# A one-core hybrid attention layer: all fetches that ScalarE issued are issued by GpSimd, and the gate's weights come in two transfers

## The chip, the cores and the metric

The kernel runs on one core of a Trainium2 chip. The metric is the device time of one execution in microseconds (us). Each version was run several times; the median counts. One execution was also taken by the hardware profiler, and the views quoted below come from it. Engines are named as in the profile: PE is TensorE's matmul, PEld its weight load, DVE is VectorE, ACT is ScalarE, POOL is GpSimd and SP is SyncE. ACTq, SPq and POOLq are the queues in which an engine issues DMAs. L145 means line 145 of the kernel.

## The reference

One layer of a model with 256 tokens of width 2048, all in fp32. The input is projected by one wide matrix; from its columns come three groups of dilated local attention (8 heads of width 128 each, with a learned bias by distance) and a gated linear attention (4 heads, decay gates from a low-rank product). Both are projected, gated, added and projected again; then a layer norm, a feed-forward part with a short convolution (width 5632), and another layer norm.

```python
parts = jnp.split(x @ w_in, cuts, axis=-1)
gq, gk, gv, gr, g_low, m_a, m_b = parts[3 * N_GROUPS:]
...
    o, lse = _dilated_group(qg, kg, vg, rel_bias[:, g * A_HEADS:(g + 1) * A_HEADS], dil)
...
ya = ya.reshape(b, s, A_WIDTH).astype(x.dtype) @ w_proj_a
log_a = jax.nn.log_sigmoid((g_low @ gla_gate_w + gla_gate_b).astype(jnp.float32)) / G_TAU
o = _gla(gq.reshape(b, s, G_HEADS, G_HK) * (G_HK ** -0.5), ..., log_a.reshape(b, s, G_HEADS, G_HK))
yb = (o.reshape(b, s, G_DV).astype(x.dtype) * jax.nn.silu(gr)) @ w_proj_b
y = jax.nn.sigmoid(m_a) * ya + jax.nn.sigmoid(m_b) * yb
return y @ w_out
```

`gla_gate_w` has 16 rows and 1024 columns: it takes the 16 low-rank columns `g_low` to the 1024 decay gates.

## The kernel before

**Weights.** The weights stream in tiles of 128 x 1024 fp32 (512 KB), issued by SP in `load` (L154). Each tile is split into two parts that TensorE takes at its faster fp32 format: ACT copies it to `whi` (L145), and DVE subtracts that copy from it to give `wlo` (L146). Every product is then three matmuls. In most places the tile is called `raw`; in the units below it is called `quarter`.

**Units.** A part of the big projection is computed with Strassen's scheme (the function around L331): seven products, named by letters after the unit's name (vA is the product A of unit v), over sums and differences of quarters of the weight matrix. The quarters are added in two ways: on DVE (L356, "quarter<-quarter,quarter"), and by a DMA that adds into its destination, issued by POOL (`add_by_dma`, L358-359, "quarter<-quarter", 120 of them). A product takes four weight tiles, four "chunks" of six matmuls. Between units stand ordinary projections, such as `gqk` or `qk` (L236 for `whi`, L238 for `wlo`).

**Side work.** Beside the stream run two lists of small stages, `side` (an attention head's steps) and `slow` (the gated linear attention), which `pump` (L194) takes up between the weight tiles. A head's `bias` (L459) fetches its bias table from DRAM in four transfers of 32 rows; `values` (L523) fetches `v`, three transfers from the buffers `vs` to which units spilled their output; `low_loads` (L584) fetches the low-rank weights: `glr`, and the gate's weights `gws`. Those lie in two tiles of 80 rows, in which rows 0-15, 32-47 and 64-79 each hold the same 16 rows of weights and the rows between are zero; so POOL clears each tile (L594) and three transfers of 16 rows fill it. `low_rank` (L615) copies its result `gl` to two more places by DMA; `get` (L666) fetches `gc` and `gq`, `att` (L711) fetches `gv`, and before the last down projection the four tiles of `acc` are fetched (L1213).

**Who issues.** In the kernel before, all these fetches are issued by ACT, `fetch` (L115) with `by=nc.scalar`. For `fetch` and `v` the issue is tied behind the newest `whi` (L120, L527, `newest` set at L145). All other fetches and all spills (L112, L573) are issued by POOL; SP issues the weight stream and the loads at the start. A scheduler decides the order of each engine's instructions from the program, and each engine then runs its own list in order: an instruction behind a DMA issue on the same engine starts only when that issue has gone out. An issue waits for the data it reads, for its destination to be free, and for one of eight slots: SP and ACT share eight, POOL has eight of its own, and the ninth issue waits until the first has landed.

Of the kernel before, what the change touches and what calls it, by code (L numbers as in the profile page):

```python
# [25 lines left out]
RANK = 16  # L26
# [34 lines left out]
def hybrid_layer(ctx: ExitStack, tc: tile.TileContext, wp, xt, wgl, gw, par, relb, onehot, rows, xk, out):  # L61
    nc = tc.nc
# [49 lines left out]
        nc.gpsimd.dma_start(d, src)  # L112
        return d

    def fetch(name, d, make=None, by=None):  # L115
        b = (make or blk)(name)
        if by is None:
            nc.gpsimd.dma_start(b, d)
        else:
            with tc.issue_after(newest[0].ins):  # L120
                by.dma_start(b, d)
        return b

    def few(name, n, bufs=4):
# [17 lines left out]
    newest = []  # L142
# [312 lines left out]
    def attend(h, qk):  # L455

        st = {}

        def bias():  # L459
            T = big("bias", (3, S))  # L460
            r = bvd[h]
            for q in range(0, P, 32):
                src = bass.AP(r.tensor, r.offset + 127 - q, [[383, 32], [32 * 384, 3], [1, S]])
                nc.scalar.dma_start(T[q : q + 32], src)
            st["T"] = T

        def scores(g):
            def f():
                if not g:
                    st["s"] = blk("s0")[:, :384], big("s1", (768,))  # L470
                q, k = qk[g][:, :S], qk[g][:, S:]
                ps = bank("ps")
                pts = []
                for t in range(2):
                    n = (t + 1) * P
                    pts.append(ps[:, t * P : t * P + n])
                    nc.tensor.matmul(pts[t], q[:, t * P : (t + 1) * P], k[:, :n], start=True, stop=True)
                for t, pt in enumerate(pts):
                    n = (t + 1) * P
                    s = st["s"][t][:, g * n : (g + 1) * n]  # L480
                    nc.vector.scalar_tensor_tensor(s, pt, scale, st["T"][:, g, S - n :], op0=ALU.mult, op1=ALU.add)
            return f

        def soft(t):
            def f():
                s = st["s"][t]
                nm = few("nm", 1)
                nc.vector.tensor_reduce(nm, s, axis=AX.X, op=ALU.max, negate=True)
                l = few("l", 1)
                nc.scalar.activation(s, s, AF.Exp, bias=nm, accum_out=l)  # L490
                rl = few("rl", 1)
                nc.vector.reciprocal(rl, l)
                nc.vector.tensor_scalar_mul(s, s, rl)
            return f

        def turn(g):
            def f():
                pt = bank("ppt")
                s0, s1 = st["s"]
                nc.tensor.transpose(pt[:, 0:P], s0[:, g * P : (g + 1) * P], ident)  # L500
                for kt in range(2):
                    c = g * S + kt * P
                    nc.tensor.transpose(pt[:, (kt + 1) * P : (kt + 2) * P], s1[:, c : c + P], ident)
                p = blk("pT")[:, :384]
                nc.scalar.activation(p, pt[:, :384], AF.Copy)
                st["p", g] = p
            return f

        def mix(g):
            def f():  # L510
                if not g:
                    st["po"] = bank("po")[:, :S]
                po, p = st["po"], st["p", g]
                v0, v1 = (st["v"][:, g, t] for t in range(2))
                nc.tensor.matmul(po, v0, p[:, :S], start=(g == 0), stop=False)
                nc.tensor.matmul(po[:, P:], v1, p[:, S:], start=False, stop=(g == 2))
                if g == 2:
                    y = tmp("ya")
                    nc.scalar.activation(y, po, AF.Copy)
                    YA[h] = spill("yas", y)  # L520
            return f

        def values():  # L523
            st["v"] = big("v", (3, 2, HD))
            for g in range(3):
                src = VS[g][h // 4][:, :, (h % 4) * HD : (h % 4 + 1) * HD]
                with tc.issue_after(newest[0].ins):  # L527
                    nc.scalar.dma_start(st["v"][:, g], src)

        idle = lambda: None  # L530
        return bias, [scores(g) for g in range(3)], [soft(0), soft(1), idle, ("values", values), turn(0), turn(1), mix(0), turn(2), mix(1), idle, mix(2)]


    VS = [[dpool.tile([P, 2, 512], F32, name=f"vs_{g}_{half}") for half in range(2)] for g in range(3)]
    GKQ = [[None] * GH for _ in range(2)]
    GV, GR = ([[None] * 2 for _ in range(GH)] for _ in range(2))
# [46 lines left out]

    def low_loads():  # L584
        glr = tmp("glr")
        nc.scalar.dma_start(glr, wgl)


        places = [slice(r, r + RANK) for r in (0, 32, 64)]
        stack = slice(0, 64 + RANK)  # L590
        gws = []
        for j in range(2):
            w = blk("gws")
            nc.gpsimd.memset(w[stack], 0.0)  # L594
            for r in places:
                nc.scalar.dma_start(w[r], gw[:, j * 512 : (j + 1) * 512])
            gws.append(w)
        gl = tmp("gl")
        nc.gpsimd.memset(gl[stack], 0.0)
        low.update(gws=gws, gl=gl, glr=glr, stack=stack, places=places)  # L600
# [14 lines left out]
    def low_rank():  # L615
        gl, stack, places = low["gl"], low["stack"], low["places"]
        glh, gll = low["parts"]
        pg = bank("pgl")
        for kc in range(16):
            w = slice(kc * RANK, (kc + 1) * RANK)  # L620
            xo = xop(kc)
            nc.tensor.matmul(pg[:RANK], glh[:, w], xo, start=(kc == 0), stop=False)
            nc.tensor.matmul(pg[:RANK, S:], gll[:, w], xo[:, :S], start=False, stop=(kc == 15))
        nc.scalar.activation(gl[:RANK], pg[:RANK, :S], AF.Copy)
        nc.vector.tensor_tensor(gl[:RANK], pg[:RANK, S:], gl[:RANK], op=ALU.add)
        for r in places[1:]:
            nc.scalar.dma_start(gl[r], gl[:RANK])

    def low_parts():
        gl, stack, places = low["gl"], low["stack"], low["places"]  # L630
# [15 lines left out]
    def gla(h):  # L646
# [17 lines left out]
            DEC[h] = spill("gcs", c)  # L664

        def get():  # L666
            st["c"] = fetch("gc", DEC[h], by=nc.scalar)
            st["q"], st["k"] = (fetch("gq", GKQ[i][h], by=nc.scalar) for i in (1, 0))

        def decay():  # L670
            c = st["c"]
# [39 lines left out]
        def att():  # L711
# [14 lines left out]
                av, av, [[0, 2], [1, P]], ALU.is_ge, 0.0, base=0, channel_multiplier=-1  # L726
            )
            st["a"] = a
            st["gv"] = [fetch("gv", d, by=nc.scalar) for d in GV[h]]

        def outs():
            a, gv = st["a"], st["gv"]
# [453 lines left out]
    for part, nf in enumerate(FSPLIT):  # L1186
# [19 lines left out]
        if nf == 4:  # L1206
            rows2 = [res("ln2", F32) for _ in range(2)]
            G2, B2 = ([row(i, n, rows2[i][:, n]) for n in range(4)] for i in range(2))
            acc = res("acc", F32)
            for n in range(2):  # L1210
                for t in range(2):
                    F[t][n] = acc[:, 2 * t + n]
                    nc.scalar.dma_start(F[t][n], ACC[t][n])  # L1213
        older = down_group(part, nf, [h() for h in hs])
    act_set(ACT_LN_EXP, held_by[0])
    norm = [mean_and_scale(t) for t in range(2)]
# [115 lines left out]
def _layout(i):  # L1332
# [9 lines left out]
        "wp": np.stack([_by_rows(f(w)[0][r : r + n], c, m) for w, r, n, c, m in STREAM]),  # L1342
        "xt": f("x")[0].T.reshape(16, P, S).transpose(1, 0, 2).reshape(P, 16 * S),
        "wgl": _by_rows(w_in, C_GL, RANK),
        "gw": f("gla_gate_w")[0],
        "par": par,
        "relb": np.concatenate([f("rel_bias"), np.ones((1, 24), np.float32)]),
        "onehot": _bucket_rows(),
# [22 lines left out]
```

## Time and profile before

| what | value |
|---|---|
| timed runs, us | 1867.16, 1867.26, 1864.41; median 1867.16 |
| span of the profiled execution, us | 1866.8 |
| queue of SP (hardware), MB, share of 16 DMA engines | 345.09, 51.6% |
| queue of POOL (software), MB, share | 118.62, 25.6% |
| queue of ACT (hardware), MB, share | 13.21, 2.2% |
| DMA issues on ACT's queue | `bias` 32, `v` 24, `gq` 8, `gv` 8, `gws` 6, `gc` 4, `acc` 4, `gl` 2, `glr` 1, and the output |

The profiled execution carries no time of its own beside its span, so the span is set against the median of the timed runs: it lies 0.36 us below it. The profile gives, for each engine, what it did and what ended the idle time before an instruction (the "releaser"). A granted clock of 1.00 is TensorE's full rate; at 0.50 each matmul takes twice as long. Busy shares are means over the span; what a change is worth in one place is read from the timelines of that place.

### The profile page before, as it was taken

Reading aid. Unit: us, or ns where it says so; the run is one execution under the profiler, and the core shown is the slowest. Engines: PE = TensorE matmul, PEld = TensorE weight load, DVE = VectorE, ACT = ScalarE, POOL = GpSimd, SP = SyncE. Lnnn points to the kernel's source line nnn. Section 1 sums busy time; section 2 is a strip of 40 time slices with the busy share of each in tenths; the row PEclk is TensorE's granted clock in tenths of the full one; section 3 lists DMA queues with packets and bytes.
Section 4 is the critical chain, followed back from the end, with each engine's and each line's share of the span. In section 5 each row is a group of like instructions: output and inputs, shape, how many; then the busy total and the mean of one; then the engine's idle time right before and its main releaser. Section 6 shows DMA issues by size and latency. Waiting matters only on the chain.

```text
span 1866.8 us, 25420 instructions
## 1 busy us (share of the span) xinstructions
PE 1819.1 (97%) x8974; PEld 1523.3 (82%) x8974; DVE 1442.1 (77%) x1715; ACT 1084.1 (58%) x1400; POOL 238.7 (13%) x361
## 2 busy tenths in 40 slices
PE   8999999999999999999999999999999999999896
PEld 6887887888887888888788868888888888888785
DVE  6978899788697978865856556886696877877878
ACT  5656586565666667646645345655565546655553
POOL 0121111111111111211300001011111110110211
PEclk9999999999999999999999999999999999999998
DMA  8898888987979798897965538569679779778782
GB/s 298 280 343 229 279 273 265 337 241 242 339 207 342 204 325 268 267 358 247 329 206 191 169 118 298 182 193 322 214 217 352 221 215 347 206 247 328 191 271 91
DMA packets 145420, 478.54 MB, mean 256 GB/s; under 512 B 17649, under 2 KB 27916, under 8 KB 145292
## 3 DMA queue, kind: packets, MB, share of 16 engines
q1 hardware_dynamic: 96764, 345.09, 51.6%
q0 software_dynamic: 34416, 118.62, 25.6%
q10 hardware_dynamic: 14112, 13.21, 2.2%
q8 instruction: 70, 1.15, 0.2%
q14 instruction: 58, 0.48, 0.1%
HBM read 382.41 MB, written 32.67 MB: 222 GB/s over the span
## 4 chain that ended last, share of the span: by engine, by line
PE 72%; issue 11%; DVE 7%; DMA 6%; ACT 2%; POOL 1%; SPq 0%; ACTq 0%; DVEq 0%; POOLq 0%
PE qk L236 9%; PE qk L238 5%; PE wd_t L273 4%; PE wd_t L272 4%; PE wd_t L274 4%; DMA raw<-in_wp 3%; DVE wlo L146 3%; PE gqk L236 3%; PE fguE L343 3%; PE fu L236 3%; PE fg L236 3%; PE fguA L343 2%; PE mD L343 2%; PE mA L343 2%; PE mE L343 2%
## 5 line engine op out<-in xcount | busy, mean ns | idle before, releaser
L146 DVE TENSOR_TENSOR wlo<-quarter,whi 128x1024 fp32r<-128x1024 f32 x484 | 578.8, 1219 | 217.1 <-issue 58.7
L145 ACT ACTIVATE whi<-quarter 128x1024 fp32r<-128x1024 f32 x484 | 504.8, 1057 | 301.0 <-DVE quarter L356 59.8
L145 ACT ACTIVATE whi<-raw 128x1024 fp32r<-128x1024 f32 (+1 forms) x346 | 358.5, 1051 | 246.8 <-DMA raw<-in_wp 121.6
L146 DVE TENSOR_TENSOR wlo<-raw,whi 128x1024 fp32r<-128x1024 f32 (+1 forms) x346 | 413.2, 1213 | 99.1 <-ACT whi L145 50.3
L236 PE MATMUL qk<-x,whi 128*128 128x512 f32 x768 | 189.2, 397 | 0.0
L359 POOL DMA_DIRECT2D quarter<-quarter x120 | 106.6, 912 | 616.4 <-DVE quarter L356 150.9
L236 PEld LDWEIGHTS qk<-x,whi 128*128 128x128 f32 x768 | 142.9, 188 | 30.2 <-issue 1.4
L356 DVE TENSOR_TENSOR quarter<-quarter,quarter 128x1024 f32<-128x1024 f32 x120 | 142.5, 1216 | 1.7 <-DMA quarter<-in_wp 1.5
L273 PE MATMUL wd_t<-wlo,h 128*128 128x512 f32 x352 | 137.4, 391 | 0.6 <-DVE wlo L146 0.6
L272 PE MATMUL wd_t<-whi,h 128*128 128x512 f32 x352 | 137.4, 393 | 0.2 <-ACT whi L145 0.2
L274 PE MATMUL wd_t<-whi,h 128*128 128x512 f32 x352 | 136.6, 389 | 0.0
L238 PEld LDWEIGHTS qk<-x,wlo 128*128 128x128 f32 x768 | 98.5, 191 | 3.7
L238 PE MATMUL qk<-x,wlo 128*128 128x256 f32 x768 | 99.6, 283 | 0.0
L236 PE MATMUL fu<-x,whi 128*128 128x512 f32 x368 | 87.9, 391 | 0.3 <-DVE gc L1045 0.3
L236 PE MATMUL fg<-x,whi 128*128 128x512 f32 x352 | 84.1, 391 | 0.0
L236 PEld LDWEIGHTS fu<-x,whi 128*128 128x128 f32 x368 | 68.3, 188 | 14.8 <-PE pt L1086 1.1
L274 PEld LDWEIGHTS wd_t<-whi,h 128*128 128x128 f32 x352 | 66.1, 188 | 14.2 <-DVE h L146 0.3
L273 PEld LDWEIGHTS wd_t<-wlo,h 128*128 128x128 f32 x352 | 66.2, 188 | 13.6 <-DVE wlo L146 0.9
L272 PEld LDWEIGHTS wd_t<-whi,h 128*128 128x128 f32 x352 | 65.9, 188 | 13.8 <-ACT whi L145 0.6
L236 PEld LDWEIGHTS fg<-x,whi 128*128 128x128 f32 x352 | 65.5, 188 | 13.3
L236 PE MATMUL gqk<-x,whi 128*128 128x512 f32 x256 | 65.3, 407 | 3.9 <-ACT whi L145 3.9
L236 PEld LDWEIGHTS gqk<-x,whi 128*128 128x128 f32 x256 | 49.5, 198 | 17.3 <-ACT whi L145 7.4
(375 smaller groups left out, 3185.2 us busy)
## 6 DMA issues: line engine op xcount, KB each, us to landing
raw<-in_wp SPq DMA_DIRECT2D x342, 512.0 KB, 6.0
quarter<-in_wp SPq DMA_DIRECT2D x304, 512.0 KB, 7.2
quarter<-quarter POOLq DMA_DIRECT2D x120, 512.0 KB, 10.1
af<-acc POOLq DMA_DIRECT2D x32, 256.0 KB, 6.9
acc<-af POOLq DMA_DIRECT2D x28, 256.0 KB, 5.7
sp<-c POOLq DMA_DIRECT2D x14, 256.0 KB, 9.5
bias<-bvd ACTq DMA_DIRECT2D x32, 96.0 KB, 6.6
v<-vs ACTq DMA_DIRECT2D x24, 128.0 KB, 4.6
```

The source lines that it names most:

```text
L145: newest[:] = [nc.scalar.activation(hi, src, AF.Copy)]
L146: nc.vector.tensor_tensor(lo, src, hi.bitcast(F32), op=ALU.subtract)
L236: nc.tensor.matmul(ps, parts(kc)[0], opnd(kc), start=(kc == 0), stop=False)
L238: nc.tensor.matmul(ps[:, S:], parts(kc)[1], opnd(kc)[:, :S], start=False, stop=(kc == nk - 1))
L272: nc.tensor.matmul(ps, xh, hi, start=first, stop=False)
L273: nc.tensor.matmul(ps, xh, lo, start=False, stop=False)
L274: nc.tensor.matmul(ps, xl, hi, start=False, stop=last)
L343: nc.tensor.matmul(ps, a(kc)[which], w[:, k * 512 : (k + 1) * 512], start=(first and w is hi and which == 0 and kc == 0), stop=(w is lo an ...
L356: tt(a, a, b, op=ALU.add)
L359: nc.gpsimd.dma_start(a, b, accum_op=ALU.add)
```

## The change

Every fetch that ACT issued is now issued by POOL: 83 transfers of `bias`, `v`, `gc`, `gq`, `gv`, `acc`, `gl` and `glr`. The tie to the newest `whi` is gone from `fetch` and `v`. The gate's weights, six transfers of 16 x 512 before, come as an array that is padded on the host with zero rows (`gw`, 80 x 1024), in two transfers of 80 x 512; the two clearings of the tiles by POOL are gone. ACT keeps one transfer, the last of the output. The kernel is four lines shorter ahead of these places, so L145 before is L141 now, L146 is L142, L356 is L352 and L359 is L355.

```diff
--- before.py
+++ after.py
@@ -112,13 +112,9 @@
         nc.gpsimd.dma_start(d, src)
         return d
 
-    def fetch(name, d, make=None, by=None):
+    def fetch(name, d, make=None):
         b = (make or blk)(name)
-        if by is None:
-            nc.gpsimd.dma_start(b, d)
-        else:
-            with tc.issue_after(newest[0].ins):
-                by.dma_start(b, d)
+        nc.gpsimd.dma_start(b, d)
         return b
 
     def few(name, n, bufs=4):
@@ -461,7 +457,7 @@
             r = bvd[h]
             for q in range(0, P, 32):
                 src = bass.AP(r.tensor, r.offset + 127 - q, [[383, 32], [32 * 384, 3], [1, S]])
-                nc.scalar.dma_start(T[q : q + 32], src)
+                nc.gpsimd.dma_start(T[q : q + 32], src)
             st["T"] = T
 
         def scores(g):
@@ -524,8 +520,7 @@
             st["v"] = big("v", (3, 2, HD))
             for g in range(3):
                 src = VS[g][h // 4][:, :, (h % 4) * HD : (h % 4 + 1) * HD]
-                with tc.issue_after(newest[0].ins):
-                    nc.scalar.dma_start(st["v"][:, g], src)
+                nc.gpsimd.dma_start(st["v"][:, g], src)
 
         idle = lambda: None
         return bias, [scores(g) for g in range(3)], [soft(0), soft(1), idle, ("values", values), turn(0), turn(1), mix(0), turn(2), mix(1), idle, mix(2)]
@@ -583,7 +578,7 @@
 
     def low_loads():
         glr = tmp("glr")
-        nc.scalar.dma_start(glr, wgl)
+        nc.gpsimd.dma_start(glr, wgl)
 
 
         places = [slice(r, r + RANK) for r in (0, 32, 64)]
@@ -591,9 +586,7 @@
         gws = []
         for j in range(2):
             w = blk("gws")
-            nc.gpsimd.memset(w[stack], 0.0)
-            for r in places:
-                nc.scalar.dma_start(w[r], gw[:, j * 512 : (j + 1) * 512])
+            nc.gpsimd.dma_start(w[stack], gw[:, j * 512 : (j + 1) * 512])
             gws.append(w)
         gl = tmp("gl")
         nc.gpsimd.memset(gl[stack], 0.0)
@@ -624,7 +617,7 @@
         nc.scalar.activation(gl[:RANK], pg[:RANK, :S], AF.Copy)
         nc.vector.tensor_tensor(gl[:RANK], pg[:RANK, S:], gl[:RANK], op=ALU.add)
         for r in places[1:]:
-            nc.scalar.dma_start(gl[r], gl[:RANK])
+            nc.gpsimd.dma_start(gl[r], gl[:RANK])
 
     def low_parts():
         gl, stack, places = low["gl"], low["stack"], low["places"]
@@ -664,8 +657,8 @@
             DEC[h] = spill("gcs", c)
 
         def get():
-            st["c"] = fetch("gc", DEC[h], by=nc.scalar)
-            st["q"], st["k"] = (fetch("gq", GKQ[i][h], by=nc.scalar) for i in (1, 0))
+            st["c"] = fetch("gc", DEC[h])
+            st["q"], st["k"] = (fetch("gq", GKQ[i][h]) for i in (1, 0))
 
         def decay():
             c = st["c"]
@@ -726,7 +719,7 @@
                 av, av, [[0, 2], [1, P]], ALU.is_ge, 0.0, base=0, channel_multiplier=-1
             )
             st["a"] = a
-            st["gv"] = [fetch("gv", d, by=nc.scalar) for d in GV[h]]
+            st["gv"] = [fetch("gv", d) for d in GV[h]]
 
         def outs():
             a, gv = st["a"], st["gv"]
@@ -1210,7 +1203,7 @@
             for n in range(2):
                 for t in range(2):
                     F[t][n] = acc[:, 2 * t + n]
-                    nc.scalar.dma_start(F[t][n], ACC[t][n])
+                    nc.gpsimd.dma_start(F[t][n], ACC[t][n])
         older = down_group(part, nf, [h() for h in hs])
     act_set(ACT_LN_EXP, held_by[0])
     norm = [mean_and_scale(t) for t in range(2)]
@@ -1342,7 +1335,7 @@
         "wp": np.stack([_by_rows(f(w)[0][r : r + n], c, m) for w, r, n, c, m in STREAM]),
         "xt": f("x")[0].T.reshape(16, P, S).transpose(1, 0, 2).reshape(P, 16 * S),
         "wgl": _by_rows(w_in, C_GL, RANK),
-        "gw": f("gla_gate_w")[0],
+        "gw": np.concatenate([np.pad(f("gla_gate_w")[0], ((0, n), (0, 0))) for n in (RANK, RANK, 0)]),
         "par": par,
         "relb": np.concatenate([f("rel_bias"), np.ones((1, 24), np.float32)]),
         "onehot": _bucket_rows(),
```

The scheduler orders each engine anew. ACT around the low-rank loads, where unit v2 computes vA and vD (names are output<-input with buffer numbers), before:

```order
L264 ACTIVATE pa_1269<-gqk_1236 128x256
L145 ACTIVATE whi_1401<-quarter_1337 128x1024
L145 ACTIVATE whi_1411<-quarter_1339 128x1024
L264 ACTIVATE pa_1320<-gqk_1286 128x256
L586 DMA glr_1323<-in_wgl 128x256
L596 DMA gws_1325<-in_gw 16x512 x3
L596 DMA gws_1330<-in_gw 16x512 x3
L369 ACTIVATE s_1386<-vA_1345 128x512
L145 ACTIVATE whi_1421<-quarter_1341 128x1024
L145 ACTIVATE whi_1431<-quarter_1343 128x1024
L145 ACTIVATE whi_1446<-raw_1444 128x1024
```

and now:

```order
L260 ACTIVATE pa_1269<-gqk_1236 128x256
L141 ACTIVATE whi_1395<-quarter_1331 128x1024
L141 ACTIVATE whi_1405<-quarter_1333 128x1024
L260 ACTIVATE pa_1320<-gqk_1286 128x256
L141 ACTIVATE whi_1415<-quarter_1335 128x1024
L141 ACTIVATE whi_1425<-quarter_1337 128x1024
L141 ACTIVATE whi_1440<-raw_1438 128x1024
L365 ACTIVATE s_1380<-vA_1339 128x512
```

The seven DMAs are gone from ACT's list, and the copy of vA (`s`) has moved behind the four `whi` of vD and a raw `whi`.

DVE at the same place, before:

```order
L146 TENSOR_TENSOR wlo_1402<-quarter_1337,whi_1401 128x1024
L146 TENSOR_TENSOR wlo_1412<-quarter_1339,whi_1411 128x1024
L356 TENSOR_TENSOR quarter_1337<-quarter_1337,quarter_1494 128x1024
L356 TENSOR_TENSOR quarter_1339<-quarter_1339,quarter_1496 128x1024
L146 TENSOR_TENSOR wlo_1422<-quarter_1341,whi_1421 128x1024
L146 TENSOR_TENSOR wlo_1432<-quarter_1343,whi_1431 128x1024
L146 TENSOR_TENSOR wlo_1447<-raw_1444,whi_1446 128x1024
L146 TENSOR_TENSOR wlo_1453<-raw_1450,whi_1452 128x1024
L356 TENSOR_TENSOR quarter_1341<-quarter_1341,quarter_1498 128x1024
L356 TENSOR_TENSOR quarter_1343<-quarter_1343,quarter_1500 128x1024
```

and now:

```order
L142 TENSOR_TENSOR wlo_1396<-quarter_1331,whi_1395 128x1024
L142 TENSOR_TENSOR wlo_1406<-quarter_1333,whi_1405 128x1024
L142 TENSOR_TENSOR wlo_1416<-quarter_1335,whi_1415 128x1024
L142 TENSOR_TENSOR wlo_1426<-quarter_1337,whi_1425 128x1024
L142 TENSOR_TENSOR wlo_1441<-raw_1438,whi_1440 128x1024
L142 TENSOR_TENSOR wlo_1447<-raw_1444,whi_1446 128x1024
L352 TENSOR_TENSOR quarter_1331<-quarter_1331,quarter_1488 128x1024
L352 TENSOR_TENSOR quarter_1333<-quarter_1333,quarter_1490 128x1024
L352 TENSOR_TENSOR quarter_1335<-quarter_1335,quarter_1492 128x1024
L352 TENSOR_TENSOR quarter_1337<-quarter_1337,quarter_1494 128x1024
```

The first two additions of quarters stood between the four `wlo` of vD; they have moved behind those and behind the two raw `wlo`.

POOL around unit gv0 and the first head's `v` and `bias`, before:

```order
L573 DMA vs_0_110<-c_311_2579 128x512
L359 DMA quarter_2793<-quarter_2899 128x1024
L573 DMA vs_0_110<-u_2343 128x512
L359 DMA quarter_2795<-quarter_2901 128x1024
L359 DMA quarter_2797<-quarter_2903 128x1024
L359 DMA quarter_2799<-quarter_2905 128x1024
L359 DMA quarter_2680<-quarter_3167 128x1024
```

and now:

```order
L568 DMA vs_0_110<-u_2337 128x512
L355 DMA quarter_2789<-quarter_2895 128x1024
L523 DMA v_2889<-vs_0_106 128x2x128
L523 DMA v_2889<-vs_0_108 128x2x128
L523 DMA v_2889<-vs_0_110 128x2x128
L460 DMA bias_3223<-bvd 32x3x256
L355 DMA quarter_2791<-quarter_2897 128x1024
L355 DMA quarter_2793<-quarter_2899 128x1024
L460 DMA bias_3223<-bvd 32x3x256 x3
L355 DMA quarter_2674<-quarter_3161 128x1024
```

The three fetches of `v` and the four of `bias` have come into POOL's list, among the accumulations of four quarters: before, quarters 2793 to 2799 with one spill between them; now, quarters 2787 (just ahead of these rows) to 2793, with three `v` and one `bias` ahead of the last two and three `bias` behind.

## The prediction

> **What bounds the kernel now.** I read the page first, for the engine that fills the span.
>
> ```profile
> span 1866.8 us, 25420 instructions
> PE 1819.1 (97%) x8974; PEld 1523.3 (82%) x8974; DVE 1442.1 (77%) x1715; ACT 1084.1 (58%) x1400; POOL 238.7 (13%) x361
> PE 72%; issue 11%; DVE 7%; DMA 6%; ACT 2%; POOL 1%; SPq 0%; ACTq 0%; DVEq 0%; POOLq 0%
> ```
>
> TensorE is busy 97% of the span. The change alters no matmul, so it can win only where TensorE stands still, and what its restart costs. The chain of waits charges DMA issues on ScalarE's queue (ACTq) with 0%, yet that share hides places where an ACT conversion (`whi`, L145) waits behind an issue: the chain then names ACT or the DMA. The view of waits for ACT lists them, as total us, times, and the longest one:
>
> ```profile
> ACT whi L145 <- DMA v<-vs: 18.0, 3, 9.2
> ACT s L369 <- DMA gws<-in_gw: 8.9, 1, 8.9
> ```
>
> The two instructions do not read `v` or `gws`; they stand behind an issue in ACT's program order. I took every stall of TensorE over 1 us from its timeline and looked at what ACT did there. ACT's own issues are behind only two of them, and these make up the sum.
>
> **Place 1, unit v2 with the low-rank loads.** TensorE's timeline (start us, duration us, operation, count, and in brackets the idle time before it):
>
> ```profile
> 144.31 0.61 PE L343 MATMUL vD<-wlo,comb 128*128 128x512 f32 x2
> ...
> 148.02 2.07 PE L343 MATMUL vD<-whi,comb 128*128 128x512 f32 x4 [3.10 <-ACT whi L145]
> ...
> 153.31 4.10 PE L236 MATMUL gqk<-x,whi 128*128 128x512 f32 x16
> 157.24 2.08 PE L238 MATMUL gqk<-x,wlo 128*128 128x256 f32 x16
> 159.16 1.09 PE L343 MATMUL vB<-whi,comb 128*128 128x512 f32 x4
> ...
> 160.54 1.07 PE L343 MATMUL vB<-whi,comb 128*128 128x512 f32 x4
> ```
>
> and ACT's in the same window, with its queue:
>
> ```profile
> 139.80 6.58 ACTq L596 DMA_DIRECT2D gws<-in_gw  x6
> 146.43 0.60 ACT L369 ACTIVATE s<-vA 128x512 f32<-128x512 f32 x1 [8.85 <-DMA gws<-in_gw]
> 146.92 1.99 ACT L145 ACTIVATE whi<-quarter 128x1024 fp32r<-128x1024 f32 x2
> ```
>
> The six gate-weight transfers hold ACT's program from 139.80 to 146.4, since a later one waits for earlier transfers to land. Behind them stand the copy of vA and the two `whi` that the third and fourth chunk of vD need. The windows show the second cost (length, TensorE busy with its count, then the busy time of weight loads, DVE, ACT and POOL with counts, then granted clock, DMA share, GB/s):
>
> ```profile
> 147.06:153.90 6.84, 5.88 (x14) 4.62 (x15) 5.90 (x6) 5.65 (x7) 0.00 (x0) 0.50 1.02 232
> 153.90:164.00 10.10, 10.10 (x54) 8.64 (x53) 8.73 (x9) 7.40 (x8) 0.58 (x1) 1.00 0.32 105
> ```
>
> After the 3.10 us stop the clock was 0.50 for 6.84 us. So the stop is paid twice.
>
> **Place 2, unit gv0 and the first attention head.** ACT with its queue, DVE, and TensorE:
>
> ```profile
> 298.26 8.74 ACTq L464 DMA_DIRECT2D bias<-bvd  x3
> 307.13 3.90 ACT L145 ACTIVATE whi<-quarter 128x1024 fp32r<-128x1024 f32 x4 [9.16 <-DMA v<-vs]
> ```
>
> ```profile
> 301.75 4.63 DVE L356 TENSOR_TENSOR quarter<-quarter,quarter 128x1024 f32<-128x1024 f32 x4
> ```
>
> ```profile
> 300.85 3.79 PE L236 MATMUL qk<-x,whi 128*128 128x512 f32 x16
> 304.48 2.07 PE L238 MATMUL qk<-x,wlo 128*128 128x256 f32 x16
> 308.24 1.19 PE L343 MATMUL gvB<-whi,comb 128*128 128x512 f32 x4 [1.69 <-ACT whi L145]
> ...
> 312.94 0.73 PE L343 MATMUL gvB<-wlo,comb 128*128 128x512 f32 x2 [0.45 <-DVE wlo L146]
> ```
>
> The fourth bias transfer sits on ACT until the head's first `v` has landed, 307.0, and the four `whi` of gvB wait 9.16 us behind it. TensorE feels 1.69 of them; here nothing shows half rate afterwards (4 matmuls in 1.19 us).
>
> **The change, part by part.** The diff takes all issues but the last `out` off ACT, and the row orders confirm it.
>
> *Term 1, the gate weights.* At full rate a chunk of vD takes 160.54 − 159.16 = 1.38 us, and the gqk unit takes 304.48 − 300.85 = 3.63 for its first sixteen matmuls and 159.16 − 157.24 = 1.92 for its second. Without ACT's block the third chunk starts 0.45 after 144.31, at 144.77; two chunks and gqk end at 144.77 + 2.76 + 5.55 = 153.08, where vB now starts at 159.16: **−6.1 us**, of which 3.25 are the stop and 2.8 the half clock. Is something late next? DVE is:
>
> ```profile
> 143.19 2.35 DVE L356 TENSOR_TENSOR quarter<-quarter,quarter 128x1024 f32<-128x1024 f32 x2
> 148.00 2.36 DVE L146 TENSOR_TENSOR wlo<-quarter,whi 128x1024 fp32r<-128x1024 f32 x2 [2.46 <-ACT whi L145]
> 150.28 2.35 DVE L146 TENSOR_TENSOR wlo<-raw,whi 128x1024 fp32r<-128x1024 f32 x2
> ```
>
> The new order puts vD's two `wlo` ahead of those two quarter additions. They then run from 143.2 to 145.5, the first ending at 144.4 and needed some 0.9 us after 144.77. The two raw `wlo` end at 147.8, four additions of 1.15 at 152.4, and vB's first `wlo` at 153.5, against 153.08 + 0.93 = 154.0 where it is needed. So nothing is left over; had the additions stayed ahead, the first `wlo` would come at 146.7 and about 1.0 us would remain. The value of term 1 lies between −3.2 (another stop of the length that trips the clock) and −6.1; I take −6.1, since each producer is early by its own row.
>
> *Term 2, the bias and v fetches.* qk would end at 304.48 + 1.92 = 306.40 and gvB could start there, 1.84 earlier. With `whi` early, the 0.45 before the last `wlo` goes too, but the first `wlo` can only follow the four additions, which end at 306.4, and is ready at 307.6, some 0.3 after gvB asks for it: **−2.0 us**. The bounds are 0 (if the `whi` wait for something else) and −2.3.
>
> *The other waits on ACT.* The row of `v` holds 18.0 us in three waits, of which place 2 is 9.2; in the other 8.8 us TensorE does not stand, because the conversions run ahead of it: I cost them at 0. If that cover were thin in the changed order, such waits would be worth up to two stops of 1 to 2 us, a bound of −4.
>
> *What GpSimd gets.* It takes 83 fetches and the two gate transfers, 85 DMAs more than it had, and loses two memsets. These rows price one issue.
>
> ```profile
> L359 POOL DMA_DIRECT2D quarter<-quarter x120 | 106.6, 912 | 616.4 <-DVE quarter L356 150.9 <-DMA quarter<-in_wp 146.3 <-DVE wlo L146 94.3
> L118 POOL DMA_DIRECT2D m<-sp x8 | 4.3, 538 | 5.5 <-DVE gr L889 2.4 <-DMA o<-os 1.4 <-DVE wlo L146 1.1
> ```
>
> 85 × 0.54 to 0.91 makes 46 to 77 us on an engine that is busy for 238.7 of 1866.8. In bulk that is covered by POOL's idle time; the price is only where an issue stands ahead of an accumulation that is needed soon (below). The padding that is now carried costs 2 × 160 KB where 6 × 32 KB were carried, and that is less than one accumulation of 512 KB: 0.
>
> *The fetches themselves* can land later without harm. For `v` (times, first and last start):
>
> ```profile
> L528 ACTq DMA_DIRECT2D v<-vs x24: 526/622/1403, 295.6 to 847.9; - x24
> L515 PE MATMUL po<-pT,v x48: 377/377/435, 326.6 to 871.9; 128*128 128x256 f32 x48
> ```
>
> The first `v` is issued 31 us before its first use, the last 24 us before the last use. No moved fetch waits ahead of TensorE as closely as an accumulation does.
>
> Sum: −6.1 − 2.0 = −8.1 on the profiled span, 1866.8 − 8.1 = 1858.7. The median of the timed runs, 1867.16, stands 0.36 over the span; with that the forecast is **1859.0 us**.
>
> One rule speaks against this sum. The Trainium skill, "DMA: Bandwidth & Descriptors", section "Issuing engines are not separate DMA queues", says that DMAs run on the same 16 engines whoever issues them, and that spreading the issue saves only the issuing sequencer's time, which is usually small. By it the sum would be near 0 and the time near 1867.2, since the issuing engine is not the one that bounds; the row of 8.85 us behind six `gws` speaks for a longer hold than the rule counts.
>
> **The rivals.** *1. It comes to nothing, or less than half.* An instruction freed from one wait meets another: at place 1 `whi` could then wait for its DVE addition, and a stop of about 3 us would halve the clock again. For it: 120 additions and accumulations feed the same conversions. Against it: the two additions in question end at 141.0 by DVE's order of work, before 143.19. If place 1 keeps its stop, only term 2 is left: 1866.8 − 2.0 + 0.36 = 1865.2; with term 1 at −3.2 alone 1864.0. Or only ACT's time of issuing goes, and both `whi` groups are late for reasons of their own: then TensorE gains nothing and the time stays at 1867.2. For that I hold 0.06 of this rival's chance, since ACT's rows show the two groups starting within 0.6 us of the end of the held issues.
>
> *2. More than forecast.* If the hidden waits of ACT do cost, −4 more: 1855.
>
> *3. Slower: accumulations stuck behind fetches on GpSimd.* POOL's program is in order, and it also issues the accumulating transfers (L359). At the first head:
>
> ```profile
> 287.24 0.66 POOL L573 DMA_DIRECT2D vs<-u  x1
> ...
> 295.33 0.86 POOL L359 DMA_DIRECT2D quarter<-quarter  x1 [0.85 <-DMA quarter<-in_wp]
> ```
>
> ```profile
> quarter<-quarter POOLq DMA_DIRECT2D x120, 512.0 KB, 10.1
> ```
>
> In the new order the third `v` waits on POOL for the spill of `vs` issued at 287.24 to land (some 9 us), and a bias and the last two of these accumulations stand behind it; the one now issued at 295.33 goes out at about 299.9 and lands at about 310.
>
> ```profile
> 311.20 3.90 ACT L145 ACTIVATE whi<-quarter 128x1024 fp32r<-128x1024 f32 x4
> 317.98 1.07 PE L343 MATMUL gvE<-whi,comb 128*128 128x512 f32 x4
> ```
>
> Its reader is the fourth of those four conversions, 311.20 + 2.9 = 314.1, or 312.1 with term 2 taken off. So it is just covered, by 2 us, and TensorE asks for it only at 319.3. Eight heads and the gate's fetches offer about ten such places. If the fetches' landing also pushes the accumulations behind, each place costs 1 to 2 us of stop (10 to 20 us in all at the far end), a few of them long enough to halve the clock for another 2.8; less the 8.1 gained, +4 to +9 is where I put it, **1871 to 1876**. It decides when accumulations land more than 2 us later than now at most of these heads. For it: several landings lie within 1 us of the conversion that reads them. Against it: ACT converts 2 to 4 us ahead of TensorE. The Trainium skill, "DMA: Bandwidth & Descriptors", section "Queues, rings and completion order", states that each DMA engine takes turns between queue rows and works within a ring in order; by it the fetches lose a turn of their own and stand in the accumulations' ring, which is this rival's mechanism. No row of this profile shows `v` or `bias` in that ring.
>
> *4. The change does not do what it says:* the rows in the new order leave ACT only one issue, so I give it nothing.
>
> **How the numbers follow.** About 0.2% (3.7 us) is what a measurement of this kernel can tell from no change, so the borders are 1863.4 and 1870.9. The forecast, 1856 to 1862: 0.45. More than forecast, 1852 to 1856: 0.12. Rival 1, 1862 to 1869: 0.26, of which 0.05 lies below 1863.4. Rival 3: 0.17, of which 0.16 lies above 1870.9. So faster 0.62, same 0.22, slower 0.16. The range 1853 to 1871 leaves out most of rival 3 and the far end of the second case, 0.18 together.
>
> **What would show it.** Term 1: ACT's `whi` of vD start before 144, vD has no gap, and the clock stays at 1.00 from 144 to 154. Term 2: gvB starts straight behind qk, and the ACT waits on `gws`, `v` and `bias` are gone. Rival 3: new gaps before TensorE that end with `whi` and, behind it, a landing of quarter<-quarter; the median landing of these over 12 us. Rival 1: a gap of 3 us still before vD's third chunk, with DVE or a DMA as its releaser. I am wrong if the sum of TensorE's gaps falls by less than 4 us, or if a new stop of over 2.5 us with a half clock appears behind a head.

## The result and the profile after

| | before | after |
|---|---|---|
| median, us (20 runs each) | 1868.01 | 1862.75 |
| lowest and highest, us | 1863.83 to 1873.43 | 1859.45 to 1867.49 |
| span of the profiled execution, us | 1866.8 | 1861.5 |
| GpSimd busy, us | 238.7 | 292.6 |

The ratio of after to before is 0.9971, with a 95% interval of 0.9964 to 0.9979: 5.4 us of 1868.0 were won, where 8.1 had been forecast. The page of the changed kernel shows that the work itself is the same, and that GpSimd's queue (q0) took over what ScalarE's (q10) had, in two pieces, engines and queues:

```profile
PE 1817.1 (98%) x8974; PEld 1522.2 (82%) x8974; DVE 1443.2 (78%) x1715; ACT 1089.0 (59%) x1400; POOL 292.6 (16%) x444
...
q0 software_dynamic: 39264, 131.70, 28.0%
...
q10 hardware_dynamic: 144, 0.26, 0.0%
```

GpSimd is busy for 53.9 us more, within the 46 to 77 of the forecast. Unit v2, TensorE's timeline of the changed kernel:

```profile
145.09 1.08 PE L339 MATMUL vD<-whi,comb 128*128 128x512 f32 x4
146.01 0.61 PE L339 MATMUL vD<-wlo,comb 128*128 128x512 f32 x2
146.46 1.07 PE L339 MATMUL vD<-whi,comb 128*128 128x512 f32 x4
...
149.18 3.79 PE L232 MATMUL gqk<-x,whi 128*128 128x512 f32 x16
152.81 2.08 PE L234 MATMUL gqk<-x,wlo 128*128 128x256 f32 x16
154.72 1.09 PE L339 MATMUL vB<-whi,comb 128*128 128x512 f32 x4
```

The third chunk of vD (146.46) follows the second without a gap, and from its start to that of vB are 8.26 us, where it took 11.14 (148.02 to 159.16) before. The windows of the same stretch show a clock of 1.00 (length, busy times of PE, PEld, DVE, ACT, POOL, then clock, DMA share, GB/s):

```profile
143.90:147.50 3.60, 3.60 (x17) 2.95 (x17) 3.60 (x4) 2.89 (x4) 1.50 (x3) 1.00 1.06 267
147.50:153.00 5.50, 5.50 (x27) 4.57 (x26) 5.50 (x6) 1.36 (x2) 0.00 (x0) 1.00 1.06 239
```

Unit gv0, TensorE and then ScalarE:

```profile
300.31 2.08 PE L234 MATMUL qk<-x,wlo 128*128 128x256 f32 x16
302.22 1.09 PE L339 MATMUL gvB<-whi,comb 128*128 128x512 f32 x4
303.90 0.73 PE L339 MATMUL gvB<-wlo,comb 128*128 128x512 f32 x2 [0.59 <-DVE wlo L142]
```

```profile
299.42 5.42 ACT L141 ACTIVATE whi<-quarter 128x1024 fp32r<-128x1024 f32 x5 [5.11 <-DVE quarter L352]
```

gvB starts straight behind qk. ScalarE now waits for the additions on VectorE, and the first `wlo` comes 0.59 us late, against 0.3 forecast.

Other stops are new, or longer than before. The view of waits of TensorE in the changed kernel (total us, times, longest) has them as

```profile
PE yp_t L269 <- DVE wlo L142: 2.2, 1, 2.2
PE pt L846 <- issue: 1.9, 1, 1.9
PE vE L339 <- ACT whi L141: 1.8, 1, 1.8
```

and the kernel before has

```profile
PE yp_t L273 <- DVE wlo L146: 1.9, 2, 1.6
...
PE pt L853 <- issue: 0.8, 1, 0.8
```

The first two of the changed kernel stand in the stretch of yp_t, at 895 and 884 us. The longest stop of the kernel before in that stretch, 1.60 us, came 11 us behind the place of the 2.15, and the changed kernel no longer has it. The third stop stands before the last chunk of vE in unit v1, where the kernel before had none at all:

```profile
125.29 1.19 PE L339 MATMUL vE<-whi,x 128*128 128x512 f32 x4 [1.81 <-ACT whi L141]
```

On ScalarE one sees why:

```profile
112.07 1.06 ACT L141 ACTIVATE whi<-quarter 128x1024 fp32r<-128x1024 f32 x1 [3.26 <-DMA quarter<-quarter]
116.56 1.06 ACT L141 ACTIVATE whi<-quarter 128x1024 fp32r<-128x1024 f32 x1 [3.43 <-DMA quarter<-quarter]
120.38 1.06 ACT L141 ACTIVATE whi<-quarter 128x1024 fp32r<-128x1024 f32 x1 [2.77 <-DMA quarter<-quarter]
124.19 1.06 ACT L141 ACTIVATE whi<-quarter 128x1024 fp32r<-128x1024 f32 x1 [2.74 <-DMA quarter<-quarter]
```

and in the kernel before:

```profile
110.38 1.06 ACT L145 ACTIVATE whi<-quarter 128x1024 fp32r<-128x1024 f32 x1 [0.55 <-DMA quarter<-quarter]
...
121.95 1.06 ACT L145 ACTIVATE whi<-quarter 128x1024 fp32r<-128x1024 f32 x1 [2.74 <-DMA quarter<-quarter]
```

Each of the four conversions waits for an accumulating transfer to land, and the last lands 2.2 us later than before. In the kernel before, TensorE took up the last of the four 1.1 us after its conversion had ended (121.95 + 1.06 = 123.01):

```profile
124.11 1.07 PE L343 MATMUL vE<-whi,x 128*128 128x512 f32 x4
```

GpSimd's timeline of the changed kernel gives the reason that the experiments then test:

```profile
98.92 0.57 POOL L568 DMA_DIRECT2D vs<-c  x1 [14.17 <-DVE c L389]
99.50 1.66 POOL L460 DMA_DIRECT2D bias<-bvd  x3
101.15 3.70 POOL L355 DMA_DIRECT2D quarter<-quarter  x4
```

Three of the first head's bias transfers stand ahead of the four accumulations; before, nothing stood between the spill `vs` and these:

```profile
99.93 0.57 POOL L573 DMA_DIRECT2D vs<-c  x1 [14.20 <-DVE c L393]
100.49 3.62 POOL L359 DMA_DIRECT2D quarter<-quarter  x4
```

Where the 5.3 us of the two spans went is read by comparing the start of the same matmul in both profiles (a minus is earlier than before):

| up to | time in the kernel before, us | shift, us | change by this stretch |
|---|---|---|---|
| first projections | 17 | −0.8 | −0.8 |
| third chunk of vE, unit v1 | 123 | −1.0 | −0.2 |
| gqk behind vE | 125 | +1.7 | +2.7 |
| vB behind vD and gqk, unit v2 | 159 | −4.4 | −6.1 |
| gvD, ahead of gvB, unit gv0 | 299 | −4.2 | +0.3 |
| last chunks of gvB | 313 | −6.3 | −2.1 |
| grD | 530 | −7.8 | −1.5 |
| yp_t, before its stops | 882 | −8.1 | −0.4 |
| yp_t, after them | 911 | −5.3 | +2.8 |
| end | 1867 | −5.3 | 0.0 |

(Shifts and changes are rounded one by one.)

### The profile page after: what moved, and what is told of

Same layout as the page of the kernel before. It is cut to its first block, busy times and chain, and to the rows that moved or that the text cites. A ratio compares the mean times of both kernels' runs of the same rounds, so it can differ in the third digit from the quotient of the medians.

```text
span 1861.5 us, 25435 instructions
## 1 busy us (share of the span) xinstructions
PE 1817.1 (98%) x8974; PEld 1522.2 (82%) x8974; DVE 1443.2 (78%) x1715; ACT 1089.0 (59%) x1400; POOL 292.6 (16%) x444
## 4 chain that ended last, share of the span: by engine, by line
PE 78%; DVE 9%; DMA 6%; issue 5%; ACT 2%; POOL 1%; SPq 0%; DVEq 0%; ACTq 0%; POOLq 0%
PE qk L232 9%; PE qk L234 5%; DVE wlo L142 4%; PE wd_t L269 4%; PE wd_t L270 4%; PE wd_t L268 4%; DMA raw<-in_wp 3%; PE fguE L339 3%; PE fg L232 3%; PE fu L232 3%; PE fguA L339 2%; PE mE L339 2%; PE fguD L339 2%; PE gqk L232 2%; PE pb_t L269 2%
## 5 line engine op out<-in xcount | busy, mean ns | idle before, releaser
L142 DVE TENSOR_TENSOR wlo<-quarter,whi 128x1024 fp32r<-128x1024 f32 x484 | 579.9, 1223 | 212.6 <-issue 65.4
L141 ACT ACTIVATE whi<-quarter 128x1024 fp32r<-128x1024 f32 x484 | 507.1, 1058 | 301.8 <-DVE quarter L352 79.0
L141 ACT ACTIVATE whi<-raw 128x1024 fp32r<-128x1024 f32 (+1 forms) x346 | 359.8, 1052 | 258.1 <-DMA raw<-in_wp 138.9
L142 DVE TENSOR_TENSOR wlo<-raw,whi 128x1024 fp32r<-128x1024 f32 (+1 forms) x346 | 414.7, 1217 | 101.3 <-ACT whi L141 50.3
L355 POOL DMA_DIRECT2D quarter<-quarter x120 | 109.4, 942 | 563.9 <-DMA quarter<-in_wp 133.1
L352 DVE TENSOR_TENSOR quarter<-quarter,quarter 128x1024 f32<-128x1024 f32 x120 | 142.7, 1221 | 2.3 <-DMA quarter<-in_wp 2.0
```

Source lines behind the costliest of these rows:

```text
L141: newest[:] = [nc.scalar.activation(hi, src, AF.Copy)]
L142: nc.vector.tensor_tensor(lo, src, hi.bitcast(F32), op=ALU.subtract)
L352: tt(a, a, b, op=ALU.add)
L355: nc.gpsimd.dma_start(a, b, accum_op=ALU.add)
```

## The experiments

Each run was timed beside the kernel before on the same chip; times in us are medians, ratios are to before. "Shift" is the start of a matmul against the profile of before. Theory: the two gains are ScalarE's held issues, and the loss at vE is bias standing ahead of accumulations in GpSimd's queue. Rivals: the gain is the engine's, not the number of issues; the loss is chance; the loss is the number of issues.

**The change once more (a_again).**

> The change itself once more, as the measure for the other runs of this group. My theory: the two gains (unit v2 without its stop and half clock, 5.9 us; unit gv0, 1.9 us) and the stop before the last chunk of vE near 124 us (1.8 us) are made by the order of issues and come back in this profile. The stop before a wlo of yp_t near 895 us (2.15 us, then half clock) hangs on how two streams of transfers fall together, and may be shorter or gone. Rival: the stop near 124 us is chance too. Time 0.9971 of before.

Measured 1862.56, ratio 0.9969 (0.9956 to 0.9982). The stop at vE is there again, 1.27 us long, and the shift goes up by 1.9 us over it; vD and gvB are as in the first profile (−6.1 and −2.1 in shift). From 882 to 911 us, yp_t, the repetition loses 0.4 us and the first profile 2.8, so the size of that loss belongs to the execution and not to the change alone.

**The gate alone on GpSimd (e1).**

```diff
-            nc.gpsimd.memset(w[stack], 0.0)
-            for r in places:
-                nc.scalar.dma_start(w[r], gw[:, j * 512 : (j + 1) * 512])
+            nc.gpsimd.dma_start(w[stack], gw[:, j * 512 : (j + 1) * 512])
```

`glr` goes to GpSimd as well, and the host pads `gw`.

> The kernel before with the gate's weights alone moved: the padded array in two transfers, and glr, issued by GpSimd; bias, v and the rest stay on ScalarE. My theory: vD loses its stop and its half clock (5.9 us), there is no stop near 124 us because bias is not ahead of the accumulations, and gvB keeps its stop of 1.7 us: 1861 to 1862 by the profile of before, ratio 0.9965 to 0.9973. Rival (the gain came from bias and v as much): ratio 0.999.

Measured 1861.43, ratio 0.9965 (0.9950 to 0.9979). The shift goes from −1.5 to −7.7 over vD, 6.1 us, and vE has no stop. The stop at gvB was expected to stay at 1.7 us and is only 0.6: with TensorE 6 us earlier, the same hold on ScalarE falls otherwise (this is argued, not tried). This part alone gives a ratio that can't be told from that of the whole change.

**The gate in two transfers, still on ScalarE (e2).**

```diff
-            nc.gpsimd.memset(w[stack], 0.0)
-            for r in places:
-                nc.scalar.dma_start(w[r], gw[:, j * 512 : (j + 1) * 512])
+            nc.scalar.dma_start(w[stack], gw[:, j * 512 : (j + 1) * 512])
```

> The kernel before with only the padded gate array in two transfers; they and all other fetches stay on ScalarE. My theory: what held ScalarE was the sixth transfer, which had to wait for the slot of a weight load issued near 130.6 us that landed at about 146; glr and two transfers take three slots whose loads have landed before 138, so ScalarE is not held at all, vD has no stop, and the time is that of the run with the gate alone on GpSimd: ratio 0.9960 to 0.9975. Rival (a fetch on ScalarE holds it, whatever its number): ScalarE still waits over 3 us behind gws, vD keeps its stop, ratio 0.999 to 1.000.

Measured 1861.03, ratio 0.9951 (0.9935 to 0.9968), a little better than expected. ScalarE's timeline in this run:

```profile
136.38 0.40 ACTq L586 DMA_DIRECT2D glr<-in_wgl  x1
136.61 0.36 ACT L264 ACTIVATE pa<-gqk 128x256 f32<-128x256 f32 x1
136.81 1.06 ACTq L594 DMA_DIRECT2D gws<-in_gw  x2
139.38 2.20 ACT L145 ACTIVATE whi<-quarter 128x1024 fp32r<-128x1024 f32 x2 [2.41 <-DVE quarter L356]
```

Two issues take 1.06 us where six took 6.58, and the `whi` behind them wait for VectorE, not for a DMA. The shift over vD is 6.1 us. So for the larger gain no other engine was needed: the sixth transfer had met a slot of the shared eight that a weight load still held, and two transfers do not reach that slot. The traces show the slots as the semaphore that each DMA issue names: all issues of SP and ACT use the same eight semaphores, all of GpSimd eight others. In the kernel before, the sixth `gws` waits for semaphore 111, which the weight load issued at 130.64 had used last, and goes out at 146.06; the three issues of this run use 113, 115 and 116 and are not held.

**Six transfers on GpSimd (e5).** The change, with the two clearings and six transfers of 16 rows back, issued by GpSimd.

> The change with the gate's weights as six transfers of 16 rows and two clearings again, now all on GpSimd. My theory: the stop moves from ScalarE to GpSimd, which is held until an accumulation issued just ahead has landed (about 9 us, to near 147 us), and the next two accumulations go out 4 to 6 us later; TensorE wants them only near 165 us, so they are covered and the time is that of the change within 1.5 us. Rival (slower): these accumulations come too late, a stop of over 1 us before vE near 160 us, and the time is 2 us or more over the change.

Measured 1864.04, ratio 0.9966 (0.9949 to 0.9982), that of the change. GpSimd's timeline:

```profile
143.16 1.92 POOL L591 DMA_DIRECT2D gws<-in_gw  x4 [0.19 <-issue]
147.07 0.49 POOL L591 DMA_DIRECT2D gws<-in_gw  x1 [1.99 <-DMA quarter<-quarter]
...
150.99 0.93 POOL L355 DMA_DIRECT2D quarter<-quarter  x1 [2.90 <-DVE quarter L352]
```

The last of the six is held until 147.07, as expected, but only for 2 us and not 9. The next accumulation waits for VectorE until 150.99; in the change it had gone out at 142.86, so it is 8 us later here, and TensorE still runs through vB and vE of unit v2 with no stop that the change hasn't. The hold moved to a place where it costs nothing that the trace shows. So either edit, fewer transfers or another engine, takes the stop of vD away. The stop at vE of unit v1, which this edit leaves as it is in the change, is there a third time, 1.16 us long.

**The first head's bias on ScalarE (e3), all bias on ScalarE (e4).** In the change:

```diff
-                nc.gpsimd.dma_start(T[q : q + 32], src)
+                (nc.gpsimd if h else nc.scalar).dma_start(T[q : q + 32], src)
```

and in e4 `nc.scalar` for all heads.

> The change with the first head's four bias transfers back on ScalarE. My theory: three of them stood ahead of the four accumulations of unit v1 in GpSimd's queue and made these land 2.2 us later; without them the stop before the last chunk of vE is 0 to 0.3 us instead of 1.8, and TensorE is 2.0 to 2.4 us earlier from 125 us on; at the end 0 to 2.4 us faster than the change, depending on what the streams near 890 us do with it. Rival (the accumulations came late by chance): the stop stays between 1 and 2 us and the time is that of the change.

Measured 1859.60, ratio 0.9949 (0.9931 to 0.9966), in one group with the repeated change: 3.0 us under it, with intervals that overlap. vE runs through:

```profile
123.58 1.07 PE L339 MATMUL vE<-whi,x 128*128 128x512 f32 x4
124.48 0.62 PE L339 MATMUL vE<-wlo,x 128*128 128x512 f32 x2
124.94 2.88 PE L232 MATMUL gqk<-x,whi 128*128 128x512 f32 x12
```

The gqk behind it starts at 124.94; in the repeated change it starts at 127.20. Of these 2.3 us, 0.4 are there before the stop, and 1.9 come from this place, just under the 2.0 to 2.4 expected.

> The change with all 32 bias transfers back on ScalarE; v, the gate and the rest stay on GpSimd. My theory: the stop near 124 us is gone as with the first head alone; ScalarE is not held at the first head near 298 us, since the fourth bias transfer waited for the landing of v, which now has slots of another engine: gvB starts straight behind qk. So the time is that of the run with the first head's bias on ScalarE, within 1 us. Rival (bias on ScalarE holds it by itself): ScalarE waits over 3 us behind bias near 298 us, and gvB's stop of 1.7 us is back.

Measured 1858.85, ratio 0.9948 (0.9930 to 0.9965). With `v` on GpSimd the bias no longer holds ScalarE at the first head:

```profile
288.32 0.81 ACTq L460 DMA_DIRECT2D bias<-bvd  x2
288.68 1.04 ACT L141 ACTIVATE whi<-raw 128x1024 fp32r<-128x1024 f32 x1
```

Its last two issues take 0.81 us, where three took 8.74 before, and no wait behind bias is left on ScalarE. In the kernel before, the fourth of these issues waits for the semaphore of the first `v`: that landed at 306.68, and the issue went out at 306.70.

**The first head's bias on GpSimd, but behind the accumulations (e9).**

```diff
+                    with tc.issue_after(added[0].ins):
+                        nc.gpsimd.dma_start(T[q : q + 32], src)
```

for head 0, with `added` set to the newest accumulation in `add_by_dma`.

> The change with the first head's four bias transfers still on GpSimd, but behind the accumulations of units v1 and v2 (they go out near 145 us; their first use is near 199 us). My theory: only their place ahead of the accumulations cost; the stop before the last chunk of vE is 0 to 0.3 us, as with ScalarE issuing them, and the time is that of the run with the first head's bias on ScalarE, ratio 0.994 to 0.996. Rival (any bias on GpSimd costs, by its issues or by what it shares): the stop stays over 1 us or a new one shows between 150 and 200 us.

Measured 1860.00, ratio 0.9945 (0.9932 to 0.9959). The four accumulations land at 108.2, 112.0, 115.8 and 119.7, where in the change they land at 112.0, 116.5, 120.3 and 124.1, and vE has no stop. So bias may be on GpSimd; its place ahead of the accumulations was what cost.

**The first head's bias in halves (e10).** Eight transfers of 16 rows, of which GpSimd's order again puts three ahead of the accumulations.

> The change with the first head's bias in eight transfers of 16 rows; three of them stand ahead of the four accumulations of unit v1, as before, but with half the rows. Theory by rows: what delays the accumulations is the time that the transfers ahead of them take in GpSimd's queue, about 3.0 us for three of 32 rows, so the last accumulation lands 1.2 to 1.8 us earlier than in the change and the stop of vE is 0 to 0.4 us. Theory by number: it is three issues of 0.55 us; the landings and the stop of 1.3 to 1.8 us stay.

Measured 1861.96, ratio 0.9960 (0.9948 to 0.9972). The first accumulation goes out at 101.15 as in the change, yet the last lands at 122.5, 1.6 us earlier, and the stop shrinks:

```profile
123.71 1.21 PE L339 MATMUL vE<-whi,x 128*128 128x512 f32 x4 [0.35 <-ACT whi L141]
```

It is 0.35 us against 1.81, 1.27 and 1.16 (the change twice, and e5), as the theory by rows has it. Counted from the issue of the spill `vs` ahead of them, so that different starts drop out, the last accumulation lands after 21.2 to 22.2 us with no bias ahead (before and all runs but these), 23.5 with three halves, and 24.3 to 25.2 with three whole ones (the change twice, e5). By the middles, about 2.9 us of delay for whole ones and 1.8 for halves: some 2.2 go with the rows and 0.7 with the number. Each group spreads by about 1 us and the halves are a single profile, so the split is rough.

**v alone on GpSimd (e7).**

```diff
-                with tc.issue_after(newest[0].ins):
-                    nc.scalar.dma_start(st["v"][:, g], src)
+                nc.gpsimd.dma_start(st["v"][:, g], src)
```

> The kernel before with only the 24 transfers of v on GpSimd. My theory: bias no longer waits for the landing of v at the first head, so gvB starts straight behind qk, 1.5 to 2.0 us earlier; vD keeps its stop and half clock, and there is no stop at vE near 124 us. Ratio 0.9985 to 0.9995. Rival (the fetches of v stand ahead of accumulations at the heads and cost there): ratio 1.000 or above, with new stops before whi behind the heads.

Measured 1864.57, ratio 0.9975 (0.9963 to 0.9986): more than expected. The shift is −1.9 at the start of gvB, as expected, and another −1.5 at grD (530), which nothing had priced. A third piece, 1.7 us, lies where the edit changes nothing: vD keeps a stop, of 2.78 us, but the half clock behind it lasts 3.4 us and not 6.84:

```profile
147.40:150.80 3.40, 3.21 (x8) 2.58 (x9) 3.23 (x3) 3.40 (x5) 0.00 (x0) 0.56 1.08 225
```

**The smallest set (e8): the gate in two transfers on ScalarE, v on GpSimd, all else as before.** The edits of e2 and e7 together.

> The smallest set that should take both stops away: the gate's padded array in two transfers on ScalarE, v on GpSimd, everything else as before. My theory: both gains (5.9 and 1.9 us) without the stop near 124 us; the moves of gc, gq, gv, acc, gl and bias are worth nothing by themselves. Ratio 0.9945 to 0.9965, the time of the run with all bias on ScalarE within 1.5 us. Rival (gc, gq and gv on ScalarE cost too): 2 us or more over that run.

> The smallest set (the gate in two transfers on ScalarE, v on GpSimd) once more, as the measure for this group. My theory: 1855 to 1858 us, ratio 0.993 to 0.995, and faster than the two others of this group or equal to them. Rival: its first time was a lucky one and it comes out at 0.996 or above.

Measured 1856.82, ratio 0.9931 (0.9914 to 0.9947), and in the second group 1856.59, ratio 0.9934 (0.9921 to 0.9948). Both stops and the one at grD are gone, and vE has none. This beats both kernels, by 12.5 and 13.4 us to before and, ratio against ratio, by 0.4% to the change. It is 2.0 us under e4 in the median, in different groups, on another chip and with intervals that overlap; so that gc, gq, gv, acc and gl are worth nothing by their move is not contradicted, and a small loss by it is not excluded.

## Why the prediction was right, and where its sum was off

The direction and the range held, and both named stops went as described. The median, 1862.75, lies 0.75 us beyond the forecast's own band, 1856 to 1862, in the band of rival 1; but what rival 1 named, a stop that stays at place 1, did not happen. Step by step:

1. **Term 1, −6.1: right.** 6.1 us in the table, in the repetition, and in e1 and e2. Clock, gap and the row of `whi` came as named. What the term rests on is now more exact: the hold was the slot of a weight load, met by the sixth issue (e2, e5).
2. **Term 2, −2.0: right.** 2.1 us in both profiles of the change, with 0.59 instead of 0.3 given back to VectorE's additions in the first.
3. **"I cost them at 0": held.** The other two waits behind `v` in the kernel before stand near 798 and 806 us, and no profile shifts there. The 1.5 us at grD that nobody had priced are another place. TensorE's stop there, before a `wlo`, is 0.81 us long, under the 1 us from which the prediction listed stops, and ScalarE does not wait for a `v`. It is 0.80 in e1 and e2 too, where `v` stays on ScalarE, and 0 to 0.28 in all runs with `v` on GpSimd. So it goes with the move of `v`; by which path isn't shown.
4. **"No moved fetch waits ahead of TensorE as closely as an accumulation does": true, and the wrong question.** The step that failed is the price of GpSimd's new issues, 0. Rival 3 had the mechanism, a fetch ahead of accumulations, and looked for it at the first head's `v`, where its cover held; the one place that cost was the first head's bias in unit v1. The row for it stood in the profile: before, the four conversions already waited for those very landings, one each 3.8 us, and the last was ready only 1.1 us before TensorE took it up. Against this the bias put 3.2 and 2.5 us more (the two profiles of the change against before, counted from the issue of `vs`). It cost 2.7 us in the first profile (1.8 of stop, the rest in slower starts of the matmuls beside it), 1.9 in the repetition, 1.8 in e5, 1.0 with halves, and 0.0 in every run with no bias ahead.
5. **What is lost behind 882 us was not in the sum.** The first profile loses 2.8 us from there to the end, the repetition 1.6. The two profiles of one kernel, e8, differ more: one gains 0.5 and the other loses 4.5, of which 1.9 in yp_t. So single spans differ by several us for reasons that no run here isolates, and the medians are the better measure. In yp_t, a `gr` fetch of the first profile landed 6.7 us after its issue, against 4.8 before and 4.7 in the repetition; a weight load is issued 0.5 us ahead of it in all three, so that load does not explain the difference, and the cause stays open.
6. **The step from span to time, 0.36 us.** Where an execution's time and span were both taken, the time is 1.7 to 2.2 us above the span, 1.8 in the mean. With 1.8 the forecast would have read 1860.5.

With 2.7 us added at vE (1.9 in the repetition) and 1.5 (0.9) taken off at grD, the sum −8.1 becomes −6.9 (−7.1); counted from the first projections, the profiles stand at −7.3 and −7.2 at 882 us. With what is lost behind that, and with the 0.8 (0.5) by which the first projections were early, the spans end at −5.3 and −6.2; the medians show −5.4, and the interval of the ratio is −3.9 to −6.7. That the sum missed by no more than 2.7 is in part luck, since the gain at grD hides about half of the loss at vE.

One sign that the prediction had named for being wrong did show: TensorE's idle time, its span less its busy time, fell from 47.7 to 44.4 us, by 3.3 (4.2 in the repetition), where under 4 was to count as wrong. The stops that were to go did go; the new ones took that much back. The other sign did not show: the one new stop with a half clock behind it, in yp_t, is 2.15 us long and not over 2.5.

The Trainium skill, "DMA: Bandwidth & Descriptors", section "Issuing engines are not separate DMA queues", which spoke for no change, comes out half right: e2 shows that the engine as such did not matter for the larger stop. What it leaves out is that an issue can hold its engine by a slot: 6.58 us for six issues, 1.06 for two. The same page's section "Queues, rings and completion order", by which transfers of one ring are taken in order, agrees with e9, e10 and the change: the last accumulation lands at 119.7, 122.5 and 124.1 us as none, half and all of three bias transfers stand ahead. The page says so of the rings of SP and ACT; here it is GpSimd's queue.

## What to carry to other kernels

When an engine that computes also issues transfers, look behind each issue for what it holds: count the issues in flight against the slots, and make fewer and larger transfers before moving them to another engine. Before a fetch is put into another engine's queue, look for work in that queue whose landings a consumer is already waiting for; that, not the queue's busy share, gives the price. A bundle of such moves is worth taking apart: here two parts of it, one of them kept on its engine, gave more than the whole.

## What the runs showed of the hardware

The four accumulating transfers of 512 KB in unit v1 landed one after another, 3.4 to 5.0 us apart and most often 3.8, in all of these profiles (elsewhere in the kernel some landed 2.2 to 2.5 us apart). Three bias transfers of 96 KB ahead of them delayed the last by about 2.9 us; as an estimate, their bytes alone, at the pace of the accumulations, would take 288 / 512 × 3.8 = 2.1.

A stop of 3.10 us was followed by 6.84 us at half clock, one of 2.78 us by 3.4 us, and the stop of 2.15 us in yp_t by 3.4 us; after 1.8 us at vE the clock stayed. The length of a stop does not settle it: in e3 a stop of 2.91 us near 1751 us was followed by no half clock, and in e1 3.4 us of half clock began at 522.9 behind two stops of only 0.86 and 0.80 us. The Trainium skill, "TensorE: Matmul & The Clock Gate", section "Part 1: The HAM clock gate (the "warmup" mystery)", has a free-running window of 3413 ns, and the two lengths are one and two of these. It gives one idle window of about 3.4 us as the condition; here a stop of 2.15 us was enough:

```profile
895.90:899.30 3.40, 3.40 (x9) 2.48 (x8) 3.40 (x6) 0.00 (x0) 0.54 (x1) 0.51 0.98 340
```
